# Two constant products ahead of the first product of a decoder trunk, and a longer fixed sequence on ScalarE and VectorE

## The chip, the cores and the metric

The kernel runs on one core of one Trainium2 chip. The metric is the device time of one execution in microseconds (us); it is the median of several runs. TensorE (PE in the profile) multiplies, with its weight loads shown apart as PEld; VectorE is DVE, ScalarE is ACT, GpSimd is POOL, and SyncE (SP) issues most of the transfers.

## The reference

One decoder layer over 512 tokens of width 1024, in float32: a norm, one input projection `h @ w_in` whose columns feed three mixers (short convolution, stick-breaking attention, retention) and their gates, an output projection, a cross-attention over 256 memory tokens, and a squared-ReLU MLP. What matters here is only its beginning:

```python
h = rmsnorm(x, norm_mix_g[l])
proj = h @ w_in[l]
cb, cc, ch, sq, sk, sv, rq, rk, rv, rg, gate_logits = jnp.split(proj, SPLIT_POINTS, axis=-1)
```

The first two projections that the kernel makes are `sv` (values of the stick-breaking attention) and `rv` (values of the retention), each 512 tokens by 512 columns.

## The kernel before

Every float32 product is made as three products of a fast float32 form: each operand is split into a high part and a low part, and high by high, high by low and low by high are added up in PSUM (`mm3`, L332 to L336). So each weight chunk of 128 by 1024 is loaded raw (`w_raw`, 6 buffers, L272), its high part is made by ScalarE and its low part by VectorE (`parts_of`, L104 to L114; `w_part`, 10 buffers).

The work is a list of items (`plan`, L289). `run_plan` (L302) walks through it; before an item that needs weights it calls `pump` (L281), which issues the loads and the splits of that item's chunks and of the next two (`AHEAD`, L34). The instructions so issued are then put in order by a scheduler, engine by engine, by times that it works out itself. Only between the entry and the exit of a "manual schedule" (L594, `S["head"]`) do ScalarE and VectorE keep the order in which the program issues their instructions.

The head of the program runs like this:

- `first_loads` (L579) issues the transfers on SyncE: the transposed x (`xT`, four tiles), the first four weight chunks (those of `sv`), and the plain x (`xs`, four tiles), mixed. It creates the manual schedule, which the first chunk's split enters (L151).
- `sv` has four weight chunks (numbered 0 to 3 here). Chunk 0 is split in two halves by VectorE alone (`Halves`, L143), chunks 1 to 3 in `Beside` (L160), each with two tiles of x times the norm's gain (`xg_h` by ScalarE, `xg_l` by VectorE, L612). In `Beside`, chunk 3 leaves the manual schedule (L172).
- The norm's factor of a token isn't known yet, so `sv` and `rv` are made from x times gain and scaled afterwards. The sum of squares of each of four token tiles is an item (`x_sum`, L616, ScalarE), `x_rs` (L620) makes the factors `rstd` from the four sums (VectorE, then GpSimd, L529), and `sv_done` (L661) takes the four token tiles of `sv` out of PSUM: for each tile two halves, and for each half a high part by ScalarE (L328) and then a low part by VectorE (L329).
- `rv` has four weight chunks too and four token tiles; `rv_done` (L670) takes each out by ScalarE. Products of `sv` and `rv` go to the four PSUM banks with the tag `mm` (L58), so a token tile of `rv` starts when a bank is free: when both halves of a token tile of `sv` have been read.
- `x_spread` (L625) spreads the factors along the tokens: VectorE makes four diagonal blocks `dg`, and TensorE multiplies them by ones (L630, float32, result `rsp`). `hT_part` (L633) then makes the normed x: VectorE twice (`xT`, L637), ScalarE a high part (`hT_h`), VectorE a low part (`hT_l`). All later projections use these.

The part of the list that the change touches:

```python
    for j in range(3):
        plan.append(sv[j])
        item(lambda j=j: x_sum(j))
    item(lambda: x_sum(3))
    item(x_rs)
    plan.append(sv[3])
    item(rv_alloc)
    rv = capture(lambda: items_m(w_in, sec(8), xg, rv_done))
    plan.append(rv[0])
    item(x_spread)
```

Of the kernel before, what the change touches and what calls it, by code (L numbers as in the profile page):

```python
# [38 lines left out]
def trunk_kernel(ctx: ExitStack, tc: tile.TileContext, x, mem, par, rot, dqd, kdec, g_mix, g_xa, g_mem, g_mlp,  # L39
                 g_fin, w_in, w_gate, w_br, w_o, w_xq, w_xk, w_xv, w_xo, w_up, w_up7, w_down, out):  # L40
    nc = tc.nc
    te, act, dve, pool = nc.tensor, nc.scalar, nc.vector, nc.gpsimd
# [18 lines left out]
    def atps(name="at"):  # L61
        return psum.tile([P, 512], F32, name=name, tag="at", bufs=4)
# [19 lines left out]
    ident = const.tile([P, P], F32, name="ident")  # L82
# [3 lines left out]
    ones = const.tile([P, 512], F32, name="ones")  # L86
# [17 lines left out]
    def parts_of(src):  # L104
        n = src.shape[1]
        part = lambda: wpool.tile([P, CW], F32R, name="w_part", bufs=WBUFS)
        if 2 * n <= CW:
            both = part()
            wh, wl = both[:, :n], both[:, n:2 * n]
        else:  # L110
            wh, wl = part(), part()
        act.copy(out=wh, in_=src)  # L112
        dve.tensor_tensor(out=wl, in0=src, in1=wh.bitcast(F32), op=ALU.subtract)  # L113
        return wh, wl  # L114
# [28 lines left out]
    class Halves(Plain):  # L143
# [6 lines left out]
        def split(self, raw):  # L150
            S["head"].__enter__()  # L151
            wh, wl = [wpool.tile([P, CW], F32R, name="w_part", bufs=WBUFS) for _ in range(2)]
            for e in range(2):
                cs = slice(e * 512, e * 512 + 512)
                dve.tensor_copy(out=wh[:, cs], in_=raw[0][:, cs])
                minus(wl[:, cs], raw[0][:, cs], wh[:, cs].bitcast(F32))
                xg_tile(e)
            return wh, wl

    class Beside(Plain):  # L160
# [6 lines left out]
        def split(self, raw):  # L167
            j = self.loads[0][1] - sec(5)
            for e in range(2):
                xg_tile(2 * j + e)  # L170
            parts = parts_of(raw[0])
            if j == 3:  # L172
                S["head"].__exit__(None, None, None)
            return parts

    class Seven:

# [113 lines left out]
    def item(fn, *chunks):  # L291
        plan.append((chunks, fn))

    def capture(build):

        n = len(plan)
        build()
        got = plan[n:]
        del plan[n:]
        return got  # L300
# [49 lines left out]
    class Mixes:  # L350
# [7 lines left out]
        def make(self, g):  # L358

            def whole(k0, t0):  # L360
                x = scr("mix", (P, 2, 256))
                hi, lo = self.a.span(k0 + 2 * g, 2, slice(t0, t0 + 256))
                dve.tensor_tensor(out=x, in0=hi.bitcast(F32), in1=lo.bitcast(F32), op=ALU.add)
                return x

            def mix(n, out, x, y, op):
                dve.tensor_tensor(out=out, in0=x, in1=y, op=op)
                h, l = self.parts[n]
                split(h[:, 2 * g:2 * g + 2, :], l[:, 2 * g:2 * g + 2, :], out)

            a11, a21 = whole(0, 0), whole(0, 256)
            mix("S3", scr("mix", (P, 2, 256)), a21, a11, ALU.subtract)
            mix("S1", a21, a21, whole(4, 256), ALU.subtract)
            mix("S2", a11, a11, a21, ALU.subtract)
            a12 = whole(4, 0)
            mix("S4", a12, a12, a11, ALU.subtract)
# [35 lines left out]
    class Pairs:  # L412
# [7 lines left out]
        def make(self, e, s, u):  # L420

            def put(names, src):
                w = unit("pr", (P, 2, 2, 256))
                split(w[:, 0], w[:, 1], src)
                for i, n in enumerate(names):
                    self.w[e][n] = w[:, 0, i, :], w[:, 1, i, :]

            def neg(out, a, b):
                dve.scalar_tensor_tensor(out=out, in0=a, scalar=-1.0, in1=b, op0=ALU.mult, op1=ALU.subtract)  # L429

            v = scr("pr_v", (P, 2, 256))
            minus(v, s, u[:, 0:1, :].broadcast_to([P, 2, 256]))
            put(("A11", "A22"), s)
            neg(u[:, 0, :], s[:, 0, :], v[:, 1, :])
            put(("S3", "S1"), v)
            hi, lo = self.w[e]["A12"] = self.b[:, e, 0, :], self.b[:, e, 1, :]
            split(hi, lo, u[:, 1, :])
            neg(u[:, 1, :], u[:, 1, :], u[:, 0, :])
            put(("S2", "S4"), u)
# [69 lines left out]
    def items_m(src, c0, a, done, nt=NT, kind=(Plain,)):  # L509

        pss = []
        for i in range(4):
            def fn(w, i=i):
                if i == 0 and kind[0] is Halves:
                    pss.extend(mmps() for t in range(nt))
                    proj_first(pss, w, a())
                    return
                for t in range(nt):
                    if i == 0:
                        pss.append(mmps())  # L520
                    proj_m(pss[t], [w], a(), t, 2 * i, 8)
                    if i == 3:
                        done(t, pss[t])
            item(fn, (kind[min(i, len(kind) - 1)], src, c0 + i))
# [47 lines left out]
    S = {}  # L572
# [39 lines left out]
    def xg_tile(k):  # L612
        hi, lo = S["xg"](k)
        split_scaled(hi, lo, S["xT"][k // 2][:, k % 2, :], gmx[:, k:k + 1])
# [24 lines left out]
        split(S["hT"].h[j], S["hT"].l[j], xT)  # L639

    xg = lambda: S["xg"]
    item(first_loads)

    hT = lambda: S["hT"]
# [36 lines left out]
    item(rv_alloc)  # L681
    rv = capture(lambda: items_m(w_in, sec(8), xg, rv_done))
    plan.append(rv[0])
    item(x_spread)
    for j in range(4):
        item(lambda j=j: hT_part(j))
# [739 lines left out]
```

## Time and profile before

| | |
|---|---|
| median of 3 runs | 1015.85 us (1015.78 to 1020.2) |
| the profiled execution, its own time | 1020.61 us |
| its span | 1018.9 us |
| TensorE busy | 996.0 us (98%) |
| VectorE busy | 718.2 us (70%) |
| ScalarE busy | 526.3 us (52%) |
| GpSimd busy | 72.7 us (7%) |
| read from memory | 109.08 MB |

Times of the trace count from the start of the span. In a timeline, a row gives the start, the length, the engine, the line, the operation, its output and inputs, how many there are of it in a row, and in brackets how long the engine stood idle ahead of it and what ended that. The view of waits names for each engine and line whom it waited for, the total in us, how often, and the longest. The view of stretches gives for each stretch its length, then TensorE's busy time and the number of its instructions, the granted clock as a share of full speed, the share of time that the transfer engines were busy, and GB/s. Spans of one engine overlap a little, since the next instruction starts before the last one has written all of its result.

### The profile page before, as it was taken

The page shows a single profiled execution, that of the slowest core. Times are in us where ns is not written, and L with a number is a line of the kernel's source. Part 1 is how long each engine was busy: PE and PEld are TensorE (multiplying, and loading weights), DVE is VectorE, ACT ScalarE, POOL GpSimd, SP SyncE. Part 2 cuts the span into 40 slices and gives each one's busy share as a digit, 9 for nine tenths or more (in the row PEclk, how much of TensorE's full clock was granted, in tenths as well). Part 3 has the DMA queues.
Part 4 walks back from the last instruction along what each step waited for, and adds up shares of the span by engine and source line. Part 5 has one row for each costly group of instructions (what it writes and reads, how often), then busy time and mean ns, then how long its engine had stood idle before and what let it go on. Part 6 is the DMA issues. An engine that isn't in the chain of part 4 may idle for free. (4 is left out here: it accounts for less than half of the span.)

```text
span 1018.9 us, 13126 instructions
## 1 busy us (share of the span) xinstructions
PE 996.0 (98%) x4958; PEld 841.2 (83%) x4958; DVE 718.2 (70%) x1066; ACT 526.3 (52%) x908; POOL 72.7 (7%) x133
## 2 busy tenths in 40 slices
PE   8999999999999999998999999999999999999996
PEld 6788888878888889987898888789888888888885
DVE  5757787778454787779795456885785786695785
ACT  6556666767422345444474445655553553553543
POOL 1001111223110000001010001000000000000001
PEclk9999999999999999999999999999999999999999
DMA  9332223212132113344444335542034125215212
GB/s 356 130 134 83 83 84 124 83 67 80 62 104 83 63 62 104 104 145 145 165 166 166 104 83 92 177 145 84 21 131 158 42 87 172 72 43 186 81 42 83
DMA packets 31888, 112.04 MB, mean 110 GB/s; under 512 B 3920, under 2 KB 3920, under 8 KB 31824
## 3 DMA queue, kind: packets, MB, share of 16 engines
q1 hardware_dynamic: 28224, 99.65, 28.5%
q0 software_dynamic: 2592, 9.44, 3.8%
q10 hardware_dynamic: 1008, 2.10, 0.6%
q8 instruction: 39, 0.64, 0.3%
q14 instruction: 25, 0.20, 0.1%
HBM read 109.08 MB, written 2.10 MB: 109 GB/s over the span
## 5 line engine op out<-in xcount | busy, mean ns | idle before, releaser
L113 DVE TENSOR_TENSOR w_part<-w_raw,w_part 128x1024 fp32r<-128x1024 f32 (+1 forms) x223 | 270.2, 1213 | 158.3 <-ACT w_part L112 151.9
L112 ACT CAST w_part<-w_raw 128x1024 fp32r<-128x1024 f32 (+1 forms) x223 | 232.3, 1044 | 284.3 <-PE mm L335 127.0
L335 PE MATMUL mm<-hT_l,w_part 128*128 128x512 f32 (+1 forms) x736 | 281.9, 384 | 1.7 <-DVE hT_l L324 1.7
L334 PE MATMUL mm<-hT_h,w_part 128*128 128x512 f32 (+1 forms) x736 | 280.5, 384 | 1.2 <-DVE r_qk L848 1.2
L336 PE MATMUL mm<-hT_h,w_part 128*128 128x512 f32 (+1 forms) x736 | 281.5, 383 | 0.0
L466 PE MATMUL p<-w_part,pr 128*128 128x512 f32 x864 | 203.6, 392 | 1.9 <-ACT pr L323 0.9
L466 PEld LDWEIGHTS p<-w_part,pr 128*128 128x128 f32 x864 | 161.8, 189 | 37.7 <-ACT pr L323 1.6
L335 PEld LDWEIGHTS mm<-hT_l,w_part 128*128 128x128 f32 x736 | 139.4, 189 | 26.8 <-DVE hT_l L324 1.9
L336 PEld LDWEIGHTS mm<-hT_h,w_part 128*128 128x128 f32 x736 | 139.4, 189 | 25.8
L334 PEld LDWEIGHTS mm<-hT_h,w_part 128*128 128x128 f32 x736 | 138.2, 189 | 27.1 <-DVE r_qk L848 1.9
L131 DVE TENSOR_TENSOR w_raw<-w_raw 128x1024 f32<-128x1024 f32 (+1 forms) x48 | 54.3, 1132 | 0.3
L128 DVE TENSOR_TENSOR x<-x,p 128x512 f32<-128x512 f32 x48 | 32.7, 683 | 9.5 <-PE p L466 9.5
L466 PE MATMUL p<-w_part,pr_b 128*128 128x512 f32 x144 | 36.4, 408 | 2.7 <-ACT w_part L112 1.4
L466 PEld LDWEIGHTS p<-w_part,pr_b 128*128 128x128 f32 x144 | 28.2, 197 | 9.5 <-ACT w_part L112 1.8
L739 DVE TENSOR_TENSOR_SCAN sb_suf<-ones,sb_e 128x128 f32<-128x128 f32 (+3 forms) x32 | 27.4, 857 | 9.5 <-POOL sb_e L718 8.2
L131 DVE TENSOR_TENSOR x<-x,p 128x512 f32<-128x512 f32 x36 | 24.2, 682 | 11.5 <-PE p L466 11.4
L742 ACT ACTIVATE sb_suf<-sb_suf 128x128 f32<-128x128 f32 (+3 forms) x32 | 15.1, 471 | 29.7 <-DVE sb_suf L741 29.5
L392 PE MATMUL p<-mix_h,w_part 128*128 128x256 f32 x128 | 25.0, 283 | 0.0
L535 ACT ACTIVATE xn<-x 128x512 f32<-128x512 f32 x24 | 15.1, 630 | 16.2 <-DVE x L131 8.3
L334 PE MATMUL mm<-w_part,xg_h 128*128 128x512 f32 x56 | 21.4, 391 | 1.3 <-DVE sb_v L329 1.3
L335 PE MATMUL mm<-w_part,xg_h 128*128 128x512 f32 x56 | 21.8, 389 | 0.0
L336 PE MATMUL mm<-w_part,xg_l 128*128 128x512 f32 x56 | 21.5, 389 | 0.0
(245 smaller groups left out, 1442.4 us busy)
## 6 DMA issues: line engine op xcount, KB each, us to landing
w_raw<-in_w_in_dram SPq DMA_DIRECT2D x55, 512.0 KB, 3.3
w_raw<-in_w_up_dram SPq DMA_DIRECT2D x32, 512.0 KB, 4.0
w_raw<-in_w_down_dram SPq DMA_DIRECT2D x32, 512.0 KB, 3.3
w_raw<-in_w_br_dram SPq DMA_DIRECT2D x12, 512.0 KB, 3.4
w_raw<-in_w_gate_dram SPq DMA_DIRECT2D x8, 512.0 KB, 3.3
w_raw<-in_w_o_dram SPq DMA_DIRECT2D x8, 512.0 KB, 3.6
w_raw<-in_w_xk_dram SPq DMA_DIRECT2D x8, 512.0 KB, 4.0
w_raw<-in_w_xv_dram SPq DMA_DIRECT2D x8, 512.0 KB, 3.3
```

The source lines that it names most:

```text
L112: act.copy(out=wh, in_=src)
L113: dve.tensor_tensor(out=wl, in0=src, in1=wh.bitcast(F32), op=ALU.subtract)
L128: dve.tensor_tensor(out=out, in0=a, in1=b, op=ALU.subtract)
L131: dve.tensor_tensor(out=out, in0=a, in1=b, op=ALU.add)
L334: te.matmul(ps, lh, rh, start=first, stop=False)
L335: te.matmul(ps, lh, rl, start=False, stop=False)
L336: te.matmul(ps, ll, rh, start=False, stop=last)
L392: te.matmul(ps[:, :256], x[:, k, :], y, start=first and k == 0 and i == 0, stop=k == 3 and i == 2, skip_group_check=True)
L466: te.matmul(acc[bank, i], x, y, start=p in ("P1", "P5", "P2") and j + k + m == 0, stop=j == 1 and k == 1 and m == 2, skip_group_check=True)
L535: act.activation(out=dst[:, cs], in_=src[:, cs], func=AF.Square, accum_out=ss[:, i:i + 1])
L739: dve.tensor_tensor_scan(out=suf[:, :s][:, ::-1], data0=ones[:, :s], data1=e1[:, :s][:, ::-1], initial=0.0, op0=ALU.mult, op1=ALU.add)
L742: act.activation(out=suf[:, :s], in_=suf[:, :s], func=AF.Exp)
```

## The change

Two things are done. First, an item ahead of all others makes two products of constants on TensorE: the identity (`ident`, 128 by 128) and a tile of ones (128 by 512), both float32, into a PSUM bank with the tag `at` that nothing reads. Second, the manual schedule is no longer left after chunk 3 of `sv` but by an item of its own, right after the first item of `rv`. So the sums of squares, the factors, the split of the first chunks of `rv` and the taking out of `sv` stand in the fixed order too.

```diff
@@ -168,10 +168,7 @@
             j = self.loads[0][1] - sec(5)
             for e in range(2):
                 xg_tile(2 * j + e)
-            parts = parts_of(raw[0])
-            if j == 3:
-                S["head"].__exit__(None, None, None)
-            return parts
+            return parts_of(raw[0])
 
     class Seven:
 
@@ -639,6 +636,13 @@
         split(S["hT"].h[j], S["hT"].l[j], xT)
 
     xg = lambda: S["xg"]
+    def keep_busy(n):
+
+        ps = atps("idle")
+        for i in range(n):
+            te.matmul(ps, ident, ones, start=i == 0, stop=i == n - 1)
+
+    item(lambda: keep_busy(2))
     item(first_loads)
 
     hT = lambda: S["hT"]
@@ -681,6 +685,7 @@
     item(rv_alloc)
     rv = capture(lambda: items_m(w_in, sec(8), xg, rv_done))
     plan.append(rv[0])
+    item(lambda: S["head"].__exit__(None, None, None))
     item(x_spread)
     for j in range(4):
         item(lambda j=j: hT_part(j))
```

The scheduler orders the instructions anew. On SyncE and GpSimd the order is the same as before. On ScalarE, VectorE and TensorE it differs up to the end of `rv`; after that, leaving aside the numbers of buffers, one pair on VectorE is swapped in the whole rest of the program. Lines of the changed kernel are 3 lower than before from L175 to the new item, and 4 to 5 higher behind it.

ScalarE, behind the high part of weight chunk 2 of `sv`, before (`x` with `ssx` is a sum of squares; `w_part` from `w_raw` is the high part of a weight chunk; here first chunk 3 of `sv`, then the four of `rv`; `sb_v` is the high part of half a token tile of `sv`):

```order
L618 ACTIVATE x_89,ssx_125<-x_89 128x1024
L618 ACTIVATE x_90,ssx_125<-x_90 128x1024
L328 ACTIVATE xg_h_120<-xT_88,gmx_84 128x512 x2
L112 CAST w_part_199<-w_raw_111 128x1024
L618 ACTIVATE x_91,ssx_125<-x_91 128x1024
L618 ACTIVATE x_92,ssx_125<-x_92 128x1024
L112 CAST w_part_231<-w_raw_130 128x1024
L112 CAST w_part_267<-w_raw_132 128x1024
L112 CAST w_part_315<-w_raw_144 128x1024
L112 CAST w_part_368<-w_raw_154 128x1024
L328 ACTIVATE sb_v_126<-mm_164,rstd_263 128x4x64
```

The same place on ScalarE in the changed kernel:

```order
L615 ACTIVATE x_92,ssx_128<-x_92 128x1024
L325 ACTIVATE xg_h_123<-xT_91,gmx_84 128x512 x2
L112 CAST w_part_202<-w_raw_114 128x1024
L615 ACTIVATE x_93,ssx_128<-x_93 128x1024
L112 CAST w_part_233<-w_raw_133 128x1024
L615 ACTIVATE x_94,ssx_128<-x_94 128x1024
L615 ACTIVATE x_95,ssx_128<-x_95 128x1024
L112 CAST w_part_269<-w_raw_135 128x1024
L325 ACTIVATE sb_v_129<-mm_167,rstd_265 128x4x64
L325 ACTIVATE sb_v_131<-mm_167,rstd_265 128x4x64
```

The third and fourth sums of squares stand behind the first chunk of `rv` now, and the taking out of `sv` begins after two chunks of `rv` and not after four.

VectorE, where it works on the normed x (`xT`, `hT_l`) and on the last token tiles of `sv` (low parts, `sb_v`), before; the last token tile of `sv` lies in the bank `mm_167`:

```order
L637 SCALAR_TENSOR_TENSOR xT_87<-xT_87,gmx_84,rsp_352 128x512
L637 SCALAR_TENSOR_TENSOR xT_88<-xT_88,gmx_84,rsp_352 128x512 x2
L329 SCALAR_TENSOR_TENSOR sb_v_127<-mm_167,rstd_263,sb_v_127 128x4x64
L324 TENSOR_TENSOR hT_l_358<-xT_85,hT_h_354 128x1024
L324 TENSOR_TENSOR hT_l_359<-xT_86,hT_h_355 128x1024
L324 TENSOR_TENSOR hT_l_360<-xT_87,hT_h_356 128x1024
L329 SCALAR_TENSOR_TENSOR sb_v_129<-mm_167,rstd_263,sb_v_129 128x4x64
```

VectorE in the changed kernel, from the end of the third token tile of `sv`; its last token tile lies in `mm_170`:

```order
L326 SCALAR_TENSOR_TENSOR sb_v_132<-mm_169,rstd_265,sb_v_132 128x4x64
L634 SCALAR_TENSOR_TENSOR xT_88<-xT_88,gmx_84,rsp_355 128x512 x2
L634 SCALAR_TENSOR_TENSOR xT_89<-xT_89,gmx_84,rsp_355 128x512 x2
L326 SCALAR_TENSOR_TENSOR sb_v_130<-mm_170,rstd_265,sb_v_130 128x4x64
L634 SCALAR_TENSOR_TENSOR xT_90<-xT_90,gmx_84,rsp_355 128x512 x2
L634 SCALAR_TENSOR_TENSOR xT_91<-xT_91,gmx_84,rsp_355 128x512 x2
L321 TENSOR_TENSOR hT_l_361<-xT_88,hT_h_357 128x1024
L321 TENSOR_TENSOR hT_l_362<-xT_89,hT_h_358 128x1024
L326 SCALAR_TENSOR_TENSOR sb_v_132<-mm_170,rstd_265,sb_v_132 128x4x64
L113 TENSOR_TENSOR w_part_318<-w_raw_147,w_part_317 128x1024
L321 TENSOR_TENSOR hT_l_363<-xT_90,hT_h_359 128x1024
L113 TENSOR_TENSOR w_part_372<-w_raw_157,w_part_371 128x1024
```

The last half of the last token tile stands behind two `hT_l` in place of three, and the low parts of the third and fourth chunk of `rv` (`w_part_318`, `w_part_372`) have moved behind it.

TensorE, where the last token tile of `rv` begins, before: the first product of `mm_340` is the 66th of `rv` and waits for ScalarE alone.

```order
L336 MATMUL mm_326<-w_part_368,xg_l_124 128x512
L334 MATMUL mm_326<-w_part_368,xg_h_120 128x512
L335 MATMUL mm_326<-w_part_369,xg_h_120 128x512
L334 MATMUL mm_340<-w_part_231,xg_h_117 128x512 [waits Activation_49]
L335 MATMUL mm_340<-w_part_232,xg_h_117 128x512
```

In the changed kernel:

```order
L331 MATMUL mm_321<-w_part_317,xg_h_122 128x512 [waits Activation_49]
L331 MATMUL mm_328<-w_part_317,xg_h_122 128x512
L331 MATMUL mm_335<-w_part_317,xg_h_122 128x512
L331 MATMUL mm_342<-w_part_233,xg_h_120 128x512 [waits DVE_49,PE_49]
L332 MATMUL mm_342<-w_part_234,xg_h_120 128x512
```

The last token tile of `rv` (`mm_342`) begins with the 40th product of `rv` now and waits for VectorE and for TensorE itself; none of the three other token tiles is finished by then.

## The prediction

> **What bounds the kernel now.** The page's first part says where to look:
>
> ```profile
> PE 996.0 (98%) x4958; PEld 841.2 (83%) x4958; DVE 718.2 (70%) x1066; ACT 526.3 (52%) x908; POOL 72.7 (7%) x133
> ```
>
> TensorE is busy 98% of the span, so a change can only win what TensorE stands idle or runs slowly, 22.9 us of 1018.9 and some slow stretches; and it loses whatever makes TensorE wait. Next I read TensorE's waits up to 75 us, since the order is the same behind that.
>
> ```profile
> PE mm L507 <- DVE w_part L155: 4.9, 1, 4.9
> PE mm L334 <- DVE sb_v L329: 1.3, 1, 1.3
> ```
>
> There are two: the start, and one for a low part of `sb_v`, that is for a PSUM bank that the taking out of `sv` has to free. TensorE's timeline shows both, and a third loss:
>
> ```profile
> 4.88 3.42 PE L507 MATMUL mm<-w_part,xg_h 128*128 128x512 f32 x8 [4.88 <-DVE w_part L155]
> 8.13 1.09 PE L507 MATMUL mm<-w_part,xg_l 128*128 128x512 f32 x4
> 9.06 1.98 PE L507 MATMUL mm<-w_part,xg_h 128*128 128x512 f32 x8
> 11.79 0.62 PE L334 MATMUL mm<-w_part,xg_h 128*128 128x512 f32 x2
> ...
> 28.16 1.02 PE L630 MATMUL rsp<-dg,ones 128*128 128x512 f32 x2
> 30.50 0.47 PE L334 MATMUL mm<-w_part,xg_h 128*128 128x512 f32 x1 [1.31 <-DVE sb_v L329]
> ...
> 52.34 0.39 PE L334 MATMUL mm<-hT_h,w_part 128*128 128x512 f32 x1
> ```
>
> The first eight products take (8.13 - 4.88) / 8 = 0.41 us each, the next four (9.06 - 8.13) / 4 = 0.23. From 11.79 to 28.16 lie the other 72 products of `sv`, 0.227 each without a gap; from 30.50 to 52.34 the 96 of `rv`, 0.2275 each, without a gap either. So whatever ends by 52.34 earlier or later moves the rest with it: what comes behind stands in the same order, and its weights are loaded ahead.
>
> **The early products.** They need constants that GpSimd makes:
>
> ```profile
> 0.98 0.52 POOL L87 MEMSET ones<- 128x512 f32 x1
> 1.55 0.28 POOL masks.py:199 TENSOR_SCALAR_AFFINE_SELECT ident<-ident 128x128 f32<-128x128 f32 x1
> ...
> 10.14 1.05 ACT L112 CAST w_part<-w_raw 128x1024 fp32r<-128x1024 f32 x1
> 11.23 1.23 DVE L113 TENSOR_TENSOR w_part<-w_raw,w_part 128x1024 fp32r<-128x1024 f32 x1 [0.20 <-ACT w_part L112]
> ```
>
> `ident` is there at 1.83, so they start at about 1.95. The same kind of product (L630) shows as two records and takes 1.02 us; pitched at the two records' 0.43 us (1.02 less the 0.59 that the last one lasts) two products are 4 x 0.43 = 1.7 us, and at the slow speed, 0.41 / 0.23 times as long, 3.1. They end between 3.7 and 5.1 to 5.4, where the first real product is ready at 4.88: a delay of 0 to 0.5 us. What they can bring: with the slow stretch gone, chunk 0's 24 products last 24 x 0.227 = 5.45 us in place of 11.79 - 4.88 = 6.9, so 1.45 us. But chunk 1's high part is there only at 10.14 + 1.05 = 11.2 and its low part, needed four products (0.9 us) later, at 12.46. So chunk 1 begins at 11.55 in effect, and of the 1.45 us 0.25 remain. From the other end, with the products late and no speed won, chunk 0 ends at 12.3. Neither reaches `rv`, whose start is set elsewhere (next part), with `sv` done by 28.7 at the latest. I take 0 us, bounds -0.25 and +0.5.
>
> The Trainium skill, in TensorE: Matmul & The Clock Gate, Part 1, says that the array starts at half its clock and gets the whole after about 3.4 us of sustained work, so two products from 1.95 would have it at full clock at about 5.4. The trace agrees with the half (0.41 against 0.23 us) and with the length (4.88 to about 7.8); by that rule alone one would write down 1.4 us won, which the rows of chunk 1 above don't let through.
>
> **The start of `rv`.** ScalarE and VectorE set it. These rows of their timelines carry it:
>
> ```profile
> 14.94 1.06 ACT L618 ACTIVATE x<-x 128x1024 f32<-128x1024 f32 x1
> 15.99 1.04 ACT L618 ACTIVATE x<-x 128x1024 f32<-128x1024 f32 x1
> 20.51 1.06 ACT L618 ACTIVATE x<-x 128x1024 f32<-128x1024 f32 x1 [0.16 <-DMA x<-in_x_dram]
> 21.90 1.05 ACT L112 CAST w_part<-w_raw 128x1024 fp32r<-128x1024 f32 x1 [0.24 <-DMA w_raw<-in_w_in_dram]
> 26.79 0.47 ACT L328 ACTIVATE sb_v<-mm,rstd 128x256 fp32r<-128x256 f32 x1
> 29.36 1.20 ACT L328 ACTIVATE sb_v<-mm,rstd 128x256 fp32r<-128x256 f32 x3 [2.10 <-DVE sb_v L329]
> 33.12 1.05 ACT L323 CAST hT_h<-xT 128x1024 fp32r<-128x1024 f32 x1 [0.19 <-DVE xT L637]
> ```
>
> ```profile
> 21.69 0.17 DVE L622 TENSOR_SCALAR msx<-ssx 128x4 f32<-128x4 f32 x1 [1.13 <-ACT x L618]
> 22.02 1.03 POOL L529 TENSOR_TENSOR rstd<-msx,half 128x4 f32<-128x4 f32 x1 [20.18 <-DVE msx L622]
> 23.09 1.31 DVE L628 TENSOR_SCALAR dg<-ident,rstd 128x128 f32<-128x128 f32 x4 [1.22 <-POOL rstd L529]
> 24.32 4.61 DVE L113 TENSOR_TENSOR w_part<-w_raw,w_part 128x1024 fp32r<-128x1024 f32 x4
> 28.85 0.47 DVE L329 SCALAR_TENSOR_TENSOR sb_v<-mm,rstd,sb_v 128x256 fp32r<-128x256 f32 x1
> 29.86 1.27 DVE L329 SCALAR_TENSOR_TENSOR sb_v<-mm,rstd,sb_v 128x256 fp32r<-128x256 f32 x3 [0.54 <-ACT sb_v L328]
> 31.69 2.71 DVE L637 SCALAR_TENSOR_TENSOR xT<-xT,gmx,rsp 128x512 f32<-128x512 f32 x4
> 38.87 3.49 DVE L324 TENSOR_TENSOR hT_l<-xT,hT_h 128x1024 fp32r<-128x1024 f32 x3
> 42.27 0.48 DVE L329 SCALAR_TENSOR_TENSOR sb_v<-mm,rstd,sb_v 128x256 fp32r<-128x256 f32 x1
> ```
>
> Before, VectorE splits four chunks (4.61 us) ahead of its first low part of `sb_v` at 28.85; the second, at 29.86, ends at 30.33 and frees the first bank, and TensorE goes on at 30.50. A token tile goes ScalarE, VectorE, ScalarE, VectorE: the second high part (29.36) waited for the first low part.
>
> Now the third and fourth sum stand behind `rv`'s first chunk, which lands no earlier than before (SyncE's order is the same): its high part runs 21.90 to 22.95. Sums follow each other at 15.99 - 14.94 = 1.05 us and with the last one's read of the result take 2.15, so `msx` starts at 25.1 where it started at 21.69. From `msx` to `dg` it took 23.09 - 21.69 = 1.4: the factors are there at 26.5. VectorE splits the second chunk of `rv` meanwhile (high part about 24.95 to 26.0, low part to 27.2, at 4.61 / 4 = 1.15), then makes `dg` (1.23 to its next instruction), and starts `sb_v` at about 28.4: 0.45 us earlier than 28.85, since two splits of 1.15 are gone from ahead of it and the sums are 3.4 later. TensorE's spread (L630) waits for `dg` until 28.4 and a little more, ends by about 29.6, and hides. **`rv` starts 0.45 us earlier, at 30.05.** With sums or the landing off by some tenths it is 0 to 0.8.
>
> **The last token tile of `rv`.** It now begins with the 40th product, so TensorE gets there at 30.05 + 39 x 0.2275 = 38.9. It needs the bank of the last token tile of `sv`, and so VectorE's last low part. VectorE's row of instructions to there, from 28.4: three token tiles at 1.0 us from low part to low part (29.86 - 28.85) and 0.4 between tiles, 4.2 us, to 32.6; four `xT` at 0.66 (2.71 for four, with 0.74 for the last), 2.65, to 35.25; one low part, 0.4, to 35.65; four `xT`, 2.65, to 38.3; two `hT_l` at 1.13 (3.49 for three), 2.25, to 40.55; the last low part, 0.47, to 41.0. ScalarE does not hold it up: its part of that half comes after the two high parts of `hT`, which end 1.05 and two tenths behind their `xT`, by 36.4. TensorE goes on 0.17 later (30.50 - 30.33), at 41.2: **a wait of 2.3 us that wasn't there.** Before, the tile began with the 66th product, at 30.50 + 65 x 0.2275 = 45.3, and the last low part was done at 42.75. Bounds: the wait is 1.5 to 3.0 if my chain is off by 0.75 either way, and 0 only if VectorE's order does not bind.
>
> Behind it nothing new is late: the low part of `rv`'s third chunk is done at 42.2, needed by the 13th product after the wait, at 44.2; the fourth chunk's at 44.4, needed at 48.7.
>
> **The clock.** A wait of 2.3 us may also cost clock. I cut the span into stretches of 3.41 us, the step between changes of the granted clock:
>
> ```profile
> 28.26:31.68 3.42, 2.10 (x8) 1.00 0.84 286
> 478.82:482.24 3.42, 1.48 (x6) 1.00 0.44 132
> 482.24:485.65 3.41, 2.62 (x6) 0.50 0.57 216
> 485.65:489.06 3.41, 3.41 (x9) 0.50 0.00 1
> 676.80:680.21 3.41, 1.27 (x11) 1.00 0.26 73
> 680.21:683.62 3.41, 3.41 (x16) 0.50 0.80 246
> ```
>
> After a stretch with TensorE busy 1.27 or 1.48 us the clock is at half, after one with 2.10 it is not; after one at half with 2.62 busy it stays, with 3.41 it recovers. A wait of 2.3 inside one stretch leaves 1.1. The limit lies between 1.48 and 2.10 busy, 1.94 and 1.31 idle; at its middle, 1.62, a stretch laid anywhere meets that much of the wait in (1.1 + 2 x 0.7) / 3.41 = 7 cases of 10. So more likely than not one stretch runs at half clock, and costs 3.41 / 2 = 1.7 us.
>
> **The sum.** 0 for the early products, -0.45 for the start of `rv`, +2.3 for the new wait, +1.7 for the clock: +3.55 us. The profiled execution took 1020.61, its span 1018.9 and 1.7 around it, and lies 4.8 above the median of the runs, 1015.85; the three half-clock stretches above cost it about 3 x 1.7 = 5.1, so I take the faster runs to have fewer of them. Against the profiled time the sum is 1024.2, against the median 1015.85 + 3.55 = 1019.4, which I give.
>
> **Rivals.**
> *No half clock.* The wait comes, the clock holds: 1015.85 + 1.85 = 1017.7. For it: 3 of 10 positions, and the limit isn't known closer than 1.31 to 1.94 idle. The Trainium skill, in TensorE: Matmul & The Clock Gate, Why this matters for your kernels, says that only a whole idle window of about 3 us brings half the clock back. The two rows that fell to half with 1.48 and 1.27 of 3.4 busy speak against that, so I give it the smaller share.
> *No wait.* VectorE and ScalarE come through faster, or the bank isn't the one I think: only the earlier start is left, 0.45 us, so 1015.4. Against it: the wait for VectorE printed at that instruction, and 2.3 us is much for a chain of measured durations to miss.
> *Two stretches at half.* The wait straddles two stretches, or what is left of it keeps the second under the 2.62 that did not suffice: 1015.85 + 1.85 + 3.4 = 1021.1, slower. It decides if the first stretch holds 1.3 idle and the second 0.8 or more, 2.1 together, just within 2.3.
> *The early products do nothing.* That is in my sum: the time is the same with and without them.
>
> **How the numbers follow.** My forecast gets 0.45, the held clock 0.25, no wait 0.15, two stretches 0.10, and 0.05 is for what I don't see. The range reaches from just under "no wait" to just over two stretches: 1015.2 to 1021.4. About 0.5% (5.1 us) is what a measurement of this kernel can tell from no change, since its own runs span 4.4 us. Faster by that would need 1010.8, more than all waits of the head together: 0.02. Slower needs 1020.9: two stretches, or a median that falls among runs like the one at 1020.2, 0.13. The rest, 0.85, is no change.
>
> **What would show it.** Right: a wait of TensorE of about 2.3 us at about 39 for a low part of `sb_v`, `rv` from about 30.0 to 54.1 or 55.8, `msx` at about 25.1, chunk 1 of `sv` at 11.5 to 12.3 with the products before it at one speed or two, and a granted clock of half in the stretch behind 41. Wrong: no wait at the last tile of `rv`, or `hT_h` products starting before 52.3; then my order of VectorE's work doesn't bind. If the waits are as said and the time is still higher, it is the clock elsewhere.

## The result and the profile after

The changed kernel took 1021.49 us (median of 11 runs, 1018.32 to 1022.86), the kernel before 1017.37 in the same comparison (11 runs, 1015.78 to 1020.71). The ratio is 1.0036, with a 95% interval of 1.0023 to 1.0048: 3.7 us slower, 2.3 to 4.9. Forecast was 1019.4, +3.55 on a median of three runs, 1015.85, that lay 1.5 us below that of the eleven; on the 1017.37 of this comparison the same +3.55 gives 1020.9.

The first part of the page and TensorE's waits up to 75 us in the changed kernel:

```profile
PE 996.8 (98%) x4962; PEld 839.5 (83%) x4962; DVE 717.6 (71%) x1066; ACT 526.1 (52%) x908; POOL 72.4 (7%) x133
```

```profile
PE mm L331 <- DVE sb_v L326: 2.5, 2, 2.1
PE idle L643 <- POOL ident masks.py:199: 1.9, 1, 1.9
```

The wait at the start is for `ident` now and 3 us shorter. Waits for low parts of `sb_v` have gone from 1.3 to 2.5, and the longer of the two is new. TensorE's timeline shows where:

```profile
1.89 3.78 PE L643 MATMUL idle<-ones,ident 128*128 128x512 f32 x4 [1.89 <-POOL ident masks.py:199]
4.98 3.11 PE L504 MATMUL mm<-w_part,xg_h 128*128 128x512 f32 x8
...
11.57 1.07 PE L331 MATMUL mm<-w_part,xg_h 128*128 128x512 f32 x4
...
28.02 1.13 PE L627 MATMUL rsp<-dg,ones 128*128 128x512 f32 x2
29.53 0.47 PE L331 MATMUL mm<-w_part,xg_h 128*128 128x512 f32 x1 [0.39 <-DVE sb_v L326]
...
40.69 0.58 PE L331 MATMUL mm<-w_part,xg_h 128*128 128x512 f32 x1 [2.07 <-DVE sb_v L326]
41.07 0.63 PE L332 MATMUL mm<-w_part,xg_h 128*128 128x512 f32 x1
...
55.31 0.39 PE L331 MATMUL mm<-hT_h,w_part 128*128 128x512 f32 x1
```

`rv` starts 0.97 us earlier (29.53 against 30.50). At its 40th product TensorE waits 2.07 us. The products behind that wait last 0.63 where others last 0.39. The first product of the normed x starts at 55.31 where it started at 52.34, 2.97 later. The granted clock, in stretches of 3.41 us, says why they are slow:

```profile
37.48:40.90 3.42, 1.35 (x7) 1.00 0.00 0
40.90:44.31 3.41, 3.41 (x9) 0.50 0.44 150
44.31:47.72 3.41, 3.41 (x16) 1.00 0.75 210
```

In the stretch with the wait TensorE is busy for 1.35 us, and the next one gets half the clock: 9 products in place of 16.

ScalarE and VectorE, in their new order, lead up to the wait. ScalarE first: chunk 1 of `sv`, the first chunk of `rv`, and the high part for the last token tile of `sv`:

```profile
10.02 1.05 ACT L112 CAST w_part<-w_raw 128x1024 fp32r<-128x1024 f32 x1
...
21.75 1.05 ACT L112 CAST w_part<-w_raw 128x1024 fp32r<-128x1024 f32 x1 [1.91 <-DMA w_raw<-in_w_in_dram]
...
35.84 0.47 ACT L325 ACTIVATE sb_v<-mm,rstd 128x256 fp32r<-128x256 f32 x1
```

```profile
24.92 0.17 DVE L619 TENSOR_SCALAR msx<-ssx 128x4 f32<-128x4 f32 x1 [0.86 <-ACT x L615]
...
27.00 0.96 DVE L625 TENSOR_SCALAR dg<-ident,rstd 128x128 f32<-128x128 f32 x4
27.88 0.47 DVE L326 SCALAR_TENSOR_TENSOR sb_v<-mm,rstd,sb_v 128x256 fp32r<-128x256 f32 x1
...
32.14 2.71 DVE L634 SCALAR_TENSOR_TENSOR xT<-xT,gmx,rsp 128x512 f32<-128x512 f32 x4
34.77 0.48 DVE L326 SCALAR_TENSOR_TENSOR sb_v<-mm,rstd,sb_v 128x256 fp32r<-128x256 f32 x1
35.16 2.71 DVE L634 SCALAR_TENSOR_TENSOR xT<-xT,gmx,rsp 128x512 f32<-128x512 f32 x4
37.80 2.35 DVE L321 TENSOR_TENSOR hT_l<-xT,hT_h 128x1024 fp32r<-128x1024 f32 x2
40.07 0.48 DVE L326 SCALAR_TENSOR_TENSOR sb_v<-mm,rstd,sb_v 128x256 fp32r<-128x256 f32 x1
```

The high part of the last half had been made at 35.84 to 36.31. Its low part stands behind four `xT` and two `hT_l` on VectorE and comes at 40.07; 0.14 us after its end TensorE goes on.

The span of this one execution is still shorter than that of the one before (1017.5 against 1018.9). That one had three stretches at half clock, at 482 to 489 and at 680; this one has only the one at 41. How many such stretches a run has differs from run to run. The mean granted clock of each run tells it: besides the slow tail after the last product, one stretch of 3.41 us lowers it by 3.41 / 2 / 1017 = 0.0017, so 0.998 is about none, 0.997 or 0.996 one, 0.995 two, 0.993 three. This is an estimate: the tail is 2.7 to 4.3 us long in the traces, and the clock is given to three digits only. Over the 94 runs of the kernel before that stood beside the experiments:

| mean clock | runs | mean time |
|---|---|---|
| 0.998 | 27 | 1016.5 us |
| 0.996, 0.997 | 46 | 1017.8 us |
| 0.995 | 20 | 1019.6 us |
| 0.993 | 1 | 1020.7 us |

That is most of the spread of this kernel's runs, and the first two groups don't overlap (1017.03 us at most, 1017.23 at least). The changed kernel has 3 runs with one stretch, 2 with two, 4 with three and 2 at 0.994 (two or three): 2.2 a run against 0.95 for the kernel before.

### The profile page after: what moved, and what is told of

Same layout as the page of the kernel before. It is cut to its first block, busy times and chain, and to the rows that moved or that the text cites. A ratio compares the mean times of both kernels' runs of the same rounds, so it can differ in the third digit from the quotient of the medians.

```text
span 1017.5 us, 13129 instructions
## 1 busy us (share of the span) xinstructions
PE 996.8 (98%) x4962; PEld 839.5 (83%) x4962; DVE 717.6 (71%) x1066; ACT 526.1 (52%) x908; POOL 72.4 (7%) x133
## 5 line engine op out<-in xcount | busy, mean ns | idle before, releaser
L747 ACT ACTIVATE sb_suf<-sb_suf 128x128 f32<-128x128 f32 (+3 forms) x32 | 15.1, 471 | 29.6 <-DVE sb_suf L746 29.4
```

Of the source, the lines that this page charges most:

```text
L747: act.activation(out=suf[:, :s], in_=suf[:, :s], func=AF.Exp)
```

## The experiments

My theory after the result: the wait at the 40th product of `rv` (2.1 us) and the half clock behind it (1.7) are the loss. Rivals: the early products cost something by themselves; the half clock has another cause; the order of the sums matters and not the bank. All ratios are to the kernel before on the same chip, with 95% intervals.

**The fixed sequence alone** (e1_sequence_alone), the changed kernel without the early products:

```diff
-    item(lambda: keep_busy(2))
```

> The long fixed sequence without the two early products; everything else stands in the changed kernel's order. My theory (the new wait at the last token tile of rv and one stretch at half clock make the whole difference, the early products nothing): as the changed kernel, 1.0036 times before (1.0023 to 1.0048), with a wait of TensorE of about 2.1 us at about 38.6 and a half-clock stretch behind it. Rival (the early products cost something of their own, such as a later start of the first real product): about 1.000 to 1.002. Rival (they win the 1.4 us of slow products, which the rest hides): 1.005.

1018.91 us, 1.0015 (1.0005 to 1.0024). So the longer sequence alone costs less than half of the change. By the clocks its runs have 1.1 half-clock stretches each, against 2.2 in the changed kernel. TensorE's timeline:

```profile
4.96 3.75 PE L504 MATMUL mm<-w_part,xg_h 128*128 128x512 f32 x8 [4.96 <-DVE w_part L155]
...
12.79 1.07 PE L331 MATMUL mm<-w_part,xg_h 128*128 128x512 f32 x4
...
39.85 0.47 PE L331 MATMUL mm<-w_part,xg_h 128*128 128x512 f32 x1 [0.83 <-DVE sb_v L326]
```

The wait at the last tile lasts 0.83 us here and not 2.07, and no stretch at half follows it. The end of the wait goes with ScalarE's start of chunk 1, which is a matter of when the transfers landed in that execution:

```profile
9.17 1.05 ACT L112 CAST w_part<-w_raw 128x1024 fp32r<-128x1024 f32 x1 [0.15 <-DMA w_raw<-in_w_in_dram]
```

From there to the end of the wait it is 39.85 - 9.17 = 30.68 us, and 40.69 - 10.02 = 30.67 in the changed kernel. Against that chain TensorE arrives later here by 2.07 - 0.83 = 1.24 us. Only a part of this is the missing products: TensorE gets to the wait 0.40 us later (39.02 against 38.62), as the clock becomes whole only at 9.81 and not at 6.76 (the trace's record of the clock) and chunk 1 begins at 12.79 against 11.57. The other 0.84 is that the chain ended sooner (39.85 against 40.69), since the transfers up to chunk 1 landed sooner in this execution. My expectation took the loss as the same with and without the early products, and that was wrong.

**The early products alone** (e2_products_alone, and the same kernel once more as e7_products_again), the kernel before with the new item:

```diff
+    item(lambda: keep_busy(2))
     item(first_loads)
```

> The two early products without the long fixed sequence; everything else stands in the order of before. My theory: the same time as before, 0.9995 to 1.0005 of it; rv starts at 30.5 with the wait of 1.3 us before it, and its last token tile waits for nothing, whatever the first 24 products gain. Rival (full clock from about 5.4 us on is worth 1.4 us): 0.9986. Rival (the early products delay the first product): 1.0005 to 1.001.

1019.76 us, 1.0021 (1.0011 to 1.0031): slower, where I expected nothing. In the head of the profiled execution nothing is lost. TensorE's timeline:

```profile
1.89 3.78 PE L646 MATMUL idle<-ones,ident 128*128 128x512 f32 x4 [1.89 <-POOL ident masks.py:199]
5.32 2.73 PE L507 MATMUL mm<-w_part,xg_h 128*128 128x512 f32 x8
...
11.53 0.84 PE L334 MATMUL mm<-w_part,xg_h 128*128 128x512 f32 x3
...
30.15 0.47 PE L334 MATMUL mm<-w_part,xg_h 128*128 128x512 f32 x1 [1.27 <-DVE sb_v L329]
```

The first product is late by 0.44 us, chunk 1 early by 0.26, and `rv` starts when VectorE lets it. So I ran it again.

> The same kernel as e2_products_alone once more (1.0021 there, with a trace that shows the head 0.34 us earlier than before and nothing lost in it). If that was chance between runs: 0.9995 to 1.0005. If the early products cost something that the one trace didn't show: 1.0011 to 1.0031 again, with a granted clock of about 0.995 in its runs where those of before mostly have 0.997 to 0.998.

1018.99 us, 1.0012 (1.0003 to 1.0022). The cost is there again, and at most a small part of it is in the head: in this trace `rv` starts at 30.22, 20.76 us after ScalarE's chunk 1 (9.46), which is 0.4 more than in e2 (30.15 - 9.80 = 20.35), because the weights of `rv`'s fourth chunk landed late. By the granted clocks, none of the 23 runs of these two reaches the 0.998 of a run without half-clock stretches, against 30 of 105 of the kernel before (its own experiment below included). Not counting 1.7 us for each stretch, they still take 0.7 us more.

**The last token tile in another bank** (e3_other_bank), the changed kernel with the last tile of `rv` in a bank of the tag `at`, which `sv` doesn't use:

```diff
-                        pss.append(mmps())
+                        pss.append(last() if last and t == nt - 1 else mmps())
...
-    rv = capture(lambda: items_m(w_in, sec(8), xg, rv_done))
+    rv = capture(lambda: items_m(w_in, sec(8), xg, rv_done, last=atps))
```

> The changed kernel, with the last token tile of rv in a PSUM bank of the other tag (at), which is free, so that it doesn't have to wait for the last token tile of sv to be taken out. The scheduler moves this tile ahead of the others by itself. My theory: the wait of 2.1 us and the half-clock stretch behind it go, and the wait of 0.4 before rv too, since six products fill it: 4.1 to 4.2 us less than the changed kernel, 0.9987 of before (0.998 to 1.0). Rival (VectorE is late for everything there, not for the bank): the wait comes back at the next thing that VectorE makes (a low part of rv's weights or of hT), and the time stays above 1.002.

1017.82 us, 0.9999 (0.9990 to 1.0009): the loss is gone. TensorE's waits up to 75 us:

```profile
PE idle L643 <- POOL ident masks.py:199: 1.9, 1, 1.9
PE mm L504 <- DVE w_part L155: 0.6, 1, 0.6
```

Neither wait for `sb_v` is there (TensorE makes nine products of the last tile ahead of those of the first), and no stretch at half follows at 41. The edit did more than change the bank: with it the scheduler orders TensorE's products anew in some twenty places up to 132 us. So the run shows that the wait goes when the tile has another bank; it doesn't part the bank from this new order.

**The clock kept** (e4_clock_kept), the changed kernel with six unread products on TensorE just ahead of the wait, all else in the same order:

```diff
     for j in range(4):
         item(lambda j=j: hT_part(j))
         plan.extend(rv[j + 1:j + 2])
+        if j == 1:
+            item(lambda: spare(6))
```

> The changed kernel, with six products of 128 by 512 (a high part of hT with itself) that nobody reads, placed on TensorE four products ahead of the one that waits; all other instructions stand in the same order on every engine. They take 6 x 0.227 = 1.36 us of a wait of 2.07, which shrinks to 0.7, and the waiting product starts when it did, at 40.7, since VectorE sets it. My theory (1.7 us of the change are a half-clock stretch that the idle time causes): 1.7 us less than the changed kernel, 1.0020 of before (1.0008 to 1.0032), with the granted clock full behind 41. Rival (the wait alone makes the difference, the clock doesn't depend on idle time of this length): as the changed kernel, 1.0036, with the half-clock stretch still there.

1018.98 us, 1.0013 (1.0001 to 1.0025). TensorE's timeline, then its clock by stretch:

```profile
37.85 1.52 PE L695 MATMUL fill<-hT_h 128*128 128x512 f32 x6
39.21 0.84 PE L331 MATMUL mm<-w_part,xg_h 128*128 128x512 f32 x3
40.73 0.47 PE L331 MATMUL mm<-w_part,xg_h 128*128 128x512 f32 x1 [0.68 <-DVE sb_v L326]
```

```profile
37.00:40.41 3.41, 3.06 (x14) 1.00 0.00 0
40.41:43.82 3.41, 3.09 (x14) 1.00 0.32 77
```

`rv`'s last tile starts no earlier than in the changed kernel (40.73 against 40.69), but with the idle time filled the clock stays whole, and 2.3 us of the loss go (1.0036 to 1.0013, give or take 1.7 us). In the traces, the first product of the normed x starts 43.72 us after ScalarE's chunk 1 (53.77 - 10.05) and not 45.29 (55.31 - 10.02), 1.57 us sooner; by the clocks the runs have 1.0 half-clock stretches each and not 2.2. Nothing else in the order differs. So idle time is what brings the half clock, and 1.7 us for it fit what goes with it.

**The sums first** (e5_sums_first), the changed kernel with the third and fourth sum and the factors ahead of chunk 2 of `sv` in the list; as the splits are issued two items ahead, this puts them ahead of the split of `rv`'s first chunk on ScalarE and VectorE. TensorE's order is that of the changed kernel:

```diff
+    for j in range(2, 4):
+        item(lambda j=j: x_sum(j))
+    item(x_rs)
+    plan.append(sv[2])
     plan.append(sv[3])
```

> The changed kernel with the four sums of squares and the factors ahead of the split of the first chunk of rv; TensorE's order is that of the changed kernel, instruction by instruction, and only five places of ScalarE's and VectorE's order before the taking out of sv differ. By the rows of the changed kernel the factors come 2.9 us earlier and the first low part of sv starts at 26.6 in place of 27.9; so the whole chain to the last low part is 1.3 us earlier. My theory (that chain sets where TensorE goes on): the last token tile of rv begins at 39.4 in place of 40.7, 1.3 us less than the changed kernel; since rv itself starts about 0.8 earlier, the wait is still about 1.6 to 1.8, and the half clock may stay: 1.0007 to 1.0025 of before. Rival (the idle time decides by itself, not the chain): as the changed kernel, 1.0036.

1019.5 us, 1.0012 (1.0002 to 1.0022). TensorE's timeline:

```profile
39.45 0.47 PE L331 MATMUL mm<-w_part,xg_h 128*128 128x512 f32 x1 [1.78 <-DVE sb_v L326]
```

The chain ends 1.1 us earlier (its chunk 1 started at 9.86; 39.45 - 9.86 = 29.6 against 30.7), and TensorE still waits 1.78 us; the clock stayed whole behind it in this execution. The rival's 1.0036 lies outside the interval. The wait belongs to VectorE's order and the bank; the sums only move it.

**A pure shift** (e8_shift_four, e9_shift_six), the kernel before with four or six unread products at the end of `rv`, to see whether the rest of the program takes a shift as it is:

```diff
+        if j == 3:
+            item(lambda: spare(4))
```

> The kernel before, with four products of 128 by 512 that nobody reads on TensorE at the end of rv, where it never waits; behind them the same order on TensorE, on VectorE one pair swapped as in the changed kernel. Everything behind comes 4 x 0.227 = 0.91 us later. If the stretches at half clock fall where they like in every run: 1.0009. If they depend on where the known waits (at about 480 and 677 us) lie against a step of 3.41 us that starts with the program: 1.0009 with up to 1.7 or 3.4 us on top or off, 0.999 to 1.004, and the granted clocks of its runs differ from those of before.

> As e8_shift_four with six such products: everything behind comes 6 x 0.227 = 1.36 us later. If the stretches at half clock fall where they like: 1.0013. If they depend on the position of the waits against a step that starts with the program: something else, 0.9995 to 1.0045, and not 0.45 us more than with four.

1020.4 us, 1.0021 (1.0009 to 1.0033), and 1020.34 us, 1.0025 (1.0016 to 1.0033). Both are about 1.2 us above the products' own time; for the six that is outside the interval, for the four at its edge. So the rest does not simply carry a shift along.

**The kernel before against itself** (e10_before_again).

> The kernel before, unchanged, against itself. If the small ratios of the early products alone (1.0021 and 1.0012) and of the products put at the end of rv (1.0021 and 1.0025) are effects of those kernels, this one gives 1.0000 and stays within 0.0007 of it. If such ratios come from the comparison itself, it lands as far off as they do. Its trace is a second look at the kernel before: at which of the known places (480, 677 to 684, and the output projection at 612 to 645 us) one execution of the same program differs from another.

1018.06 us, 1.0005 (0.9995 to 1.0014), so ratios such as 1.0021 are not the comparison's doing; a single 1.0012 could be. Its trace taught more. TensorE's waits up to 75 us, TensorE's first rows, and ScalarE's chunk 1:

```profile
PE mm L507 <- DVE w_part L155: 4.9, 1, 4.9
```

```profile
4.90 3.75 PE L507 MATMUL mm<-w_part,xg_h 128*128 128x512 f32 x8 [4.90 <-DVE w_part L155]
8.45 1.32 PE L507 MATMUL mm<-w_part,xg_l 128*128 128x512 f32 x4
```

```profile
9.47 1.05 ACT L112 CAST w_part<-w_raw 128x1024 fp32r<-128x1024 f32 x1
```

The same program: in this execution the clock became whole at 8.95 us and not at 7.78, chunk 1 was there 0.67 earlier (9.47 against 10.14), and the wait of 1.3 us ahead of `rv` was gone. So single executions of one kernel differ by more than half a microsecond in the head, and a difference of that size between two traces says nothing by itself.

**The other bank without the early products** (e11_bank_no_products) **and in the kernel before** (e12_before_bank), with the edit of e3.

> The changed kernel with the other bank for the last token tile of rv, and without the early products. No wait for VectorE is left behind the start in the run with the other bank (0.9999), so there every tenth that the early products win in the head should come through: chunk 1 of sv began at 11.57 with them and at 12.79 without. Theory of the head alone: this kernel takes 1.2 us more than the one with the products, a ratio of about 1.0011, and its products of the normed x start about 0.7 us later than in the kernel before. Rival, that the early products cost something that is not in the head: it takes no more than the one with them, a ratio of 0.9985 to 1.0000.

> The kernel before with nothing but the other bank for the last token tile of rv, whose products TensorE can then make while it waits for the first bank of sv. Theory of the head: the wait of 1.3 us ahead of rv goes, no other comes, the rest starts 1.3 us earlier: ratio 0.9987 (0.9980 to 0.9995). Rival, that any shift of the program costs about as much again later: 1.0000 or more.

1016.87 us, 0.9992 (0.9983 to 1.0001), and 1017.27 us, 0.9993 (0.9984 to 1.0002). In both traces the start is TensorE's only wait up to 75 us. The first came out on the rival's side: without the early products it is not slower than with them (0.9999). Chunk 1 began at 12.08 here and at 12.37 in e3, where its weights came late (ScalarE's split at 11.26 against 9.18), so the gain that I had put at 1.2 us was not there in those executions. Both are at best 0.8 us better than the kernel before, and no interval leaves out 1: none of these versions is shown to beat it.

## Why the prediction was right, and where it was not

**The early products, 0 us.** Up to the start of `rv` the rows bear it out: in the two traces of the kernel before `rv` starts 20.36 and 20.33 us after ScalarE's chunk 1 (30.50 - 10.14, 29.80 - 9.47), and 20.35 with the products in (30.15 - 9.80, e2), so what they win goes into a wait. But as a term of the whole time 0 was wrong. With the products the longer sequence gives 1.0036, without them 1.0015; and alone they gave 1.0021 and 1.0012. My rival "the time is the same with and without them", which I put into the sum, is refuted. Two accounts fit, and no run parts them. One is that the products make TensorE ready sooner, so that the new wait is longer and costs the clock: 2.07 us did in the changed kernel, 0.83 did not in e1. The other is that they cost as much by themselves, mostly behind the head: 1.5 us for the sequence and 1.2 to 2.1 for the products add up to 2.7 to 3.6, nearly the whole 3.7. In the two profiled executions the head does differ (the normed x 45.29 us after chunk 1 with them, 52.89 - 9.17 = 43.72 without), but there the transfers landed differently too.

**The start of `rv`, 0.45 us earlier.** It was 0.97, just outside my 0 to 0.8; counted from ScalarE's chunk 1 it was 0.85 (29.53 - 10.02 = 19.51 against 20.36). `msx` (24.92 against 25.1) and the first low part (27.88 against 28.4) came a little sooner than my chain, mostly because the four `dg` held VectorE 0.88 us (27.00 to 27.88) where I had 1.23.

**The new wait, 2.3 us.** It was 2.07 at 38.62, for the bank I had named, with the last low part done at 40.55 where I had 41.0. Both ends came 0.3 to 0.5 us sooner, so that the difference held. In e3, with another bank, it is gone; the rival "no wait" falls.

**The half clock, 1.7 us.** It came in the stretch behind 41, and e4 shows that the idle time brings it. The page of the Trainium skill that I had weighed against this (TensorE: Matmul & The Clock Gate, Why this matters for your kernels, which asks only that idle gaps stay under about 3 us) does not hold for this kernel: a wait of 2.07 us, with 1.35 of 3.41 us busy, was enough for half. "Two stretches" did not come: the stretch behind had 3.41 busy and recovered.

**The sum, +3.55.** Head of the trace: -0.97 + 2.07 + 1.7 = 2.8 of the 2.97 at 55.31. (From ScalarE's chunk 1 to the first product of the normed x it is 45.29 us against 42.20 and 42.21 in the two traces of the kernel before, so 3.1.) Over all runs, set against those of the table, the mean is 3.3 us higher: 1.2 more stretches at half, 2.1 us, and 1.2 us of the rest, where -0.97 + 2.07 would be 1.10. The measured 3.7 fits the sum, and the two terms that make it, the wait and the half clock, are the ones that e3 and e4 take away. That the total came so close is partly luck: the products were put at 0, and without them the same sequence cost 1.5 us. The level was off: at 1015.85 and 1015.78 two of my three runs lay below even the table's mean of runs without any half-clock stretch, and the median of eleven is 1.5 higher. So in plain time the measured 1021.49 lies 0.1 us above the top of my range (1021.4), while the ratio, 1.0036, is the one forecast (1019.4 / 1015.85 = 1.0035).

**What stays open.** Why the early products alone, and the shifts, cost more than the head shows. In all pairs the kernel with the products came out slower, with the other bank too (0.9999 against 0.9992, not clear of noise). Two places take part. At about 480 and 677 us TensorE waits for about the limit of the clock, so it depends on how the stretches fall whether one goes to half. And at 616 to 645 us (attention output, weights `w_xo`) a trace loses up to 2 us against another, when ScalarE splits a chunk late. ScalarE in the second run of the kernel before, and in e8:

```profile
616.25 1.05 ACT L112 CAST w_part<-w_raw 128x1024 fp32r<-128x1024 f32 x1 [1.35 <-DMA w_raw<-in_w_xo_dram]
```

```profile
619.13 2.00 ACT L112 CAST w_part<-w_raw 128x1024 fp32r<-128x1024 f32 x2 [3.06 <-PE mm L335]
```

Behind it stand the softmax of the next head and TensorE. From ScalarE's copy of `xo_s` ahead of this place (611.58 in the kernel before) to TensorE's product behind its wait (643.14) it takes 31.56 and 31.94 us in the two traces of the kernel before, 32.76 and 33.34 with the early products alone, 33.60 and 32.20 with the two shifts. So in these executions 0.8 to 1.8 us were lost here with the early products alone, far behind the head; the changed kernel, which has them too, takes 31.98 us. Why the head's edits would steer these places is shown by no run; single executions of one kernel differ there by 0.4 to 0.6 us.

## What to carry to other kernels

Ask of each engine that is made ready sooner where it will wait next: TensorE's earlier start here only ran into a wait that another engine ends, and the wait cost the clock as well. When a wait is for a bank, look first at which bank the next tile takes and what stands ahead of its last reader; one other bank, with the order that the scheduler then chose, undid the whole loss. With effects of 0.2%, compare many runs and count the half-clock stretches of each before reading a difference between two traces.

## What the hardware showed

The limit for the half clock lies closer than my prediction had it (1.48 to 2.10 us busy of 3.41). In the 13 traces, leaving out the idle end behind the last product, 16 stretches at the whole clock were followed by one at half; TensorE was busy 1.76 us or less in each. All with 1.80 or more were followed by a whole one, and of those below only two, in e5 and, with the last products of the program, in e12. The nearest to the limit in the second run of the kernel before, and the two exceptions (e5, then e12):

```profile
479.99:483.40 3.41, 1.76 (x6) 1.00 0.46 154
483.40:486.81 3.41, 3.41 (x10) 0.50 0.46 156
```

```profile
37.27:40.68 3.41, 1.63 (x8) 1.00 0.00 0
40.68:44.10 3.42, 3.42 (x17) 1.00 0.61 175
```

```profile
1007.13:1010.54 3.41, 1.50 (x7) 1.00 0.18 69
1010.54:1013.95 3.41, 0.00 (x0) 1.00 0.33 125
```

So the busy time of the records is not quite what counts; at about half a stretch, either can come. Back to the whole clock it took more: 2.62 busy did not do in the kernel before, 3.02 did in e8. And the stretches don't begin with the program: by the traces' record of the clock, it became whole at 7.78 to 10.85 us with first products at 4.88 to 5.29, and at 5.57 to 6.76 with the early products (from 1.89). The Trainium skill (TensorE: Matmul & The Clock Gate, Part 1) has the window run freely, which agrees, and moves the change to the whole clock by 0.5 us either way, where these runs show 3.1 us from first to last.
